# A threshold search moved from ScalarE to VectorE in a sparse-attention decoder layer, and the first query operands made earlier

## The chip, the core and the metric

The kernel runs on one core of one Trainium2 chip. The metric is the device time of one execution in microseconds, the median of several runs. Times inside an execution come from the hardware profile of one run; they are counted from the start of its span.

## What is computed

One decoder layer on 1024 tokens of width 1024 in float32. The part that matters here is the sparse attention. A light indexer gives each query token a score for every earlier token; only the 256 best-scored tokens take part in that query's softmax. The kernel doesn't gather: it finds, for each query row, the exact 256th score as a threshold, and adds a large negative number to the logits of all other tokens.

```python
score = jnp.einsum('bqh,bqhs->bqs', w, jax.nn.relu(logits))
score = jnp.where(causal[None], score, -jnp.inf)
_, idx = lax.top_k(score, k_sel)              # k_sel = 256
s = jnp.where(valid[:, None], s, -jnp.inf)    # s: logits of the chosen tokens
p = jax.nn.softmax(s, axis=-1)
```

Around it stand a modulation of the input, a combined projection (queries, keys, values, pooling channels, indexer), the output projection, two layer norms and a gated feed-forward block.

## The kernel before

The 1024 tokens are eight tiles of 128 rows. Tile i has 128 x (i + 1) earlier tokens; tiles 0 and 1 have 256 at most and need no search. Stages follow each other: the indexer projection, then the scores of tiles 2 to 7 (loop at line 783), then the projections of pooling channels, keys and values in 24 groups (loop at line 940), then attention, output projection, feed-forward.

**The search** (`bisect`, line 627) finds a row's threshold bit by bit: 15 rounds on the upper 16 bits of the score, a short pass in the middle, 16 rounds on the lower 16 bits, then some operations that write the row's bias over its score (lines 709 to 732). A round counts, for each tile of the stream, how many keys lie above a candidate. On VectorE (`search_v`, line 660) a round is one counting pass for each tile (`tensor_scalar` with an accumulated output) and two small updates. On ScalarE (`search_a`, line 672) it is one Sign activation for each tile with an accumulated sum, and four small updates on GpSimd (POOL), which the next round waits for. Lines 37 and 38 share the tiles out: tiles 3 and 2, then 7 and 6, on ScalarE; 5 and 4 on VectorE. A stream's middle and last steps are on VectorE in either case.

**The order of the work.** `fill` (line 761) and `advance` (line 747) are a planner that runs while the program is written. Each engine has an estimated clock; before an operation that would wait, steps of the open streams are put in, if their estimated cost fits into the wait plus a slack (line 51: 0.5 us for VectorE, 1.5 us for ScalarE). Streams opened earlier go first. The stream of 3 and 2 opens in the score loop (line 785), those of 5 and 4 and of 7 and 6 behind it (lines 813, 814). `need(i)` (line 757), called ahead of a tile's first softmax (line 1040), puts in whatever the stream of that tile still lacks.

**Attention** runs over 32 units (group g of two tiles, pair of heads, tile i; line 1020), in the order of tiles 1 and 0, then 3 and 2, 5 and 4, 7 and 6, four pairs of heads each. A unit has its scores on TensorE, a fused add-bias-and-maximum on VectorE and an exponential on ScalarE for each of two heads (`u_exp`, line 1036), a scaling on POOL, transposes on TensorE, copies by ScalarE and VectorE, and the product with the values. Scores and softmax of a unit are put into the program two units ahead of its transposes. From unit 12 on, two steps of another generator are put in with each unit (`mods`, lines 463 and 1145 to 1149): 16 products of 1024 columns and then 8 accumulations, all on VectorE, for the second half's modulation and gate.

**The query operands** (`q_make`, line 1002) are four transposes on TensorE, four copies on ScalarE and two subtractions on VectorE (`q_operands`, line 557). Those of tiles 1 and 0 are made behind the last projection group (lines 1007 to 1015); those of later tiles during attention, at the units listed in `Q_AT` (line 46). Their places (line 991) are in the areas H, W and V. The first two blocks of the output weights (`WO`, line 1096) lie in the area V, from word 4096 to 8192; the first is split by `wo_split(0)` at unit 30 in the program (line 1159).

Of the kernel before, what the change touches and what calls it, by code (L numbers as in the profile page):

```python
# [12 lines left out]
F32R = mybir.dt.float32r  # L13
# [20 lines left out]
BIG = 1.0e30  # L34
NEG = -3.0e38
NOT_TAKEN = -(2.0 ** 100)
TILES_A = ([3, 2], [7, 6])
TILES_V = [5, 4]
PIN = "VAG"
W_POOL = (1, 3)  # L40
AHEAD = 2
# [6 lines left out]
MODS = (12, 2)  # L48
Q_AT = (((0, 0), (1, 0)), ((0, 0), (1, 0)), ((1, 0), (2, 0)))
WARM = 66  # L50
SLACK = {"V": 0.5, "A": 1.5}
SYNC = 0.06
UPDATE = "G"
POOL_AT = 3
# [123 lines left out]
def decoder_layer_kernel(  # L178
# [22 lines left out]
    def buf(where, off, n, name, dt=F32):  # L201
        return nc.alloc_sbuf_tensor_at(f"{name}_{where}{off}", [P, n], dt, offset=area[where] + 4 * off).ap()
# [59 lines left out]
    def raw_slot():  # L262
        n_raw[0] += 1
        return RAW[(n_raw[0] - 1) % 3]
# [286 lines left out]
    def q_transpose(src):  # L551
        pt = psA("qT")
        for pr in range(4):
            T.transpose(pt[:, pr * P : (pr + 1) * P], src[:, pr * P : (pr + 1) * P], ident)
        return pt
# [28 lines left out]
    for c in range(2):  # L584
        pt = psA("ikT")
# [30 lines left out]
    kD = buf("T", 0, 960, "keysD")  # L616
    k4 = buf("T", 960, 320, "keys4")
    k5 = buf("T", 1280, 384, "keys5")
    junkA = buf("X", 6528, 512, "junkA").bitcast(BF16)
    junkB = buf("X", 7040, 256, "junkB").bitcast(BF16)  # L620
    colsD = buf("X", 8576, 64, "colsD")
    keys = {2: kA[:, 0:192], 3: kA[:, 192:448], 4: k4, 5: k5, 6: kD[:, 0:448], 7: kD[:, 448:960]}
    keys = {i: kw.bitcast(I16) for i, kw in keys.items()}
# [3 lines left out]
    def bisect(tiles, cols, on_act):  # L627
# [3 lines left out]
        cntc, kp, sg, cand, pr, M, ng, th, ib, thr, ahead = (col(q) for q in range(11))  # L631
        flip = ib.bitcast(I16)[:, 0:nt]
        kv = {i: keys[i] for i in tiles}
        own = (junkA if 7 in tiles else junkB) if on_act else junk7

        def trash(i):
            return own[:, 0 : P * (i + 1)]
# [100 lines left out]
    def open_stream(*a):  # L738
        pinned.update(PIN)
        b = bisect(*a)  # L740
        streams.append([T.t, next(b), b])
        times.fill = fill
# [40 lines left out]
    for i in range(2, NT):  # L783
# [26 lines left out]
                q_evac(*qpend.pop(0))  # L810
        dg = sc[:, n - P : n]
        G.affine_select(dg, dg, pattern=[[-1, P]], compare_op=ALU.is_ge, fill=NEG, base=0, channel_multiplier=1)
    open_stream(TILES_V, colsD, False)
    open_stream(TILES_A[1], colsA[:, 64:128], True)


    SP.dma_start(pscale, pscale_in)
# [90 lines left out]
    def at_(slot, f):  # L908
        late.setdefault(slot, []).append(f)
# [27 lines left out]

    PAIRS = (0, 6, 8, 14, 16)
    held, pair = {}, None
    for n_, (kind, a, b) in enumerate(groups):  # L940
        if n_ in PAIRS:
            pb = psB("pair")
            held[n_], held[n_ + 1] = pb[:, 0:512], pb[:, 512:1024]
            pair = [(held[q_], u_f(*groups[q_][1:]) if kind == "u" else t_f(groups[q_][1])) for q_ in (n_, n_ + 1)]
        if n_ in held:
            for kp in range(2):
                for pp, f in pair:
                    f(pp, [4 * (n_ not in PAIRS) + 2 * kp, 4 * (n_ not in PAIRS) + 2 * kp + 1])
        else:
            held[n_] = psA("pj")  # L950
            (u_f(a, b) if kind == "u" else t_f(a))(held[n_], range(KT))
        pp = held[n_]
        if n_ in (6, 14):
            w_loads(wk_in if n_ == 6 else wv_in)
        if n_ in (7, 8, 15, 16):
            for kp in ((0, 1) if n_ % 2 else (2, 3)):
                w_split(kp)
        nd = n_ + 2 if n_ in PAIRS else n_ + 1
        if kind == "u":
            at_(nd, lambda a=a, b=b, pp=pp: u_take(a, b, pp))  # L960
            if b == 1:
                at_(nd + 2, lambda a=a: u_split(a))
                at_(nd + 2, lambda a=a: u_split2(a))
                at_(nd + POOL_AT + 1, lambda a=a: u_pool(a))
        elif kind == "k":
            tr = n_ + (4 if n_ in PAIRS or n_ - 1 in PAIRS else 3)
            at_(nd, lambda a=a, pp=pp, tr=tr: take(a, pp, tr))
        else:
            at_(nd, lambda a=a, pp=pp: v_take(a, pp))
        if n_ == 20:  # L970
            at_(n_, lambda: gate_fin(GR, macc, 0, raw_slot()))
        for f in late.pop(n_, []):
            f()
    last = len(groups)
    pinned.clear()

# [6 lines left out]
        n_st[0] = (o + n) % 128 if o + n + n <= 128 else 0  # L983
        return stat[0][:, o : o + n]

    ptb = [[buf("H", (2 * s_ + e) * 2048, 2048, "pT").rearrange("p (j q) -> p j q", j=8) for e in (0, 1)] for s_ in (0, 1)]
    smr = buf("H", 8192, 6144, "sm")
    qabh = buf("H", 14336, 1536, "qab", F32R)
    qabw = [buf("W", 6144 - 2048 * i, 1536, "qab", F32R) for i in (0, 1)]
    qabv = [buf("V", 5120 + i * 1536, 1536, "qab", F32R) for i in (0, 1)]  # L990
    qab = {1: qabh, 0: qabw[0], 3: qabw[1], 2: qabw[0], 5: qabh, 4: qabv[0], 7: qabv[1], 6: qabh}

    qops = {}

    qraw = [buf("C", 768, 512, "qraw"), buf("X", 7552, 512, "qraw")]

    def q_load(i):
        raw = qraw[i % 2]
        SP.dma_start(raw, q_d[i])
        return raw  # L1000

    def q_make(i, raw, pt=None):
        b = qab[i]
        qops[i] = (b[:, 0:1024], b[:, 1024:1536])
        q_operands(pt if pt is not None else q_transpose(raw), *qops[i])

    for s_ in (last, last + 1):
        if s_ == last:
            qr = {i: q_load(i) for i in (1, 0)}
            qp = {i: q_transpose(qr[i]) for i in (1, 0)}  # L1010
        for f in late.pop(s_, []):
            f()
    assert not late, late
    for i in (1, 0):
        q_make(i, qr[i], qp[i])

    def cat_slot(g):
        return WS[g]
# [581 lines left out]
```

## Time and profile before

| | |
|---|---|
| median of 3 runs | 1340.32 us (1337.98 to 1340.81) |
| the profiled execution | 1340.45 us |
| its span | 1338.5 us |
| TensorE matmul busy | 1219.7 us, 91% of the span |
| VectorE (DVE) busy | 1006.4 us, 75% |
| ScalarE (ACT) busy | 592.4 us, 44% |
| GpSimd (POOL) busy | 606.0 us, 45% |
| mean granted TensorE clock | 0.95 |

A share over the whole span is an average over stages with different limits. Stages can be told apart by their rows: projections end at 343.8 us, the first softmax of tile 7 starts at 498.25 us, and from about 550 us on the output projection and the feed-forward block run. In the names, `junkA` is the scratch output of the search of tiles 7 and 6, `junkB` of 3 and 2, `junk` of 5 and 4; `colsA` and `colsD` are the small columns of candidates and counts; `keysD` are the keys of 7 and 6; `qab` is a query operand, `sm` a softmax row, `gacc` the second gate. Line 158 is the helper that issues every operation, so rows are told apart by tile names. [...]

### The profile page before, as it was taken

Reading aid. Unit: us, or ns where it says so; the run is one execution under the profiler, and the core shown is the slowest. Engines: PE = TensorE matmul, PEld = TensorE weight load, DVE = VectorE, ACT = ScalarE, POOL = GpSimd, SP = SyncE. Lnnn points to the kernel's source line nnn. Section 1 sums busy time; section 2 is a strip of 40 time slices with the busy share of each in tenths; the row PEclk is TensorE's granted clock in tenths of the full one; section 3 lists DMA queues with packets and bytes.
Section 4 is the critical chain, followed back from the end, with each engine's and each line's share of the span. In section 5 each row is a group of like instructions: output and inputs, shape, how many; then the busy total and the mean of one; then the engine's idle time right before and its main releaser. Section 6 shows DMA issues by size and latency. Waiting matters only on the chain. (4 is left out here: it accounts for less than half of the span.)

```text
span 1338.5 us, 15961 instructions
## 1 busy us (share of the span) xinstructions
PE 1219.7 (91%) x5570; PEld 958.7 (72%) x5570; DVE 1006.4 (75%) x1685; ACT 592.4 (44%) x1103; POOL 606.0 (45%) x624
## 2 busy tenths in 40 slices
PE   7978997989586849999799999999999999999996
PEld 6655676768454526788677888888888888888875
DVE  6898789889766778467887767576767767676688
ACT  2345754667888956427533223232323223232321
POOL 1393584675344536315663414152342414242557
PEclk8999999989677978999899999999999999999998
DMA  9540020221103431420121011120101112110112
GB/s 337 213 162 31 16 92 19 95 68 44 48 24 118 142 111 64 169 84 1 47 79 63 32 63 63 50 76 33 63 32 64 42 53 70 57 63 32 63 48 110
DMA packets 24997, 101.79 MB, mean 76 GB/s; under 512 B 3411, under 2 KB 3411, under 8 KB 20566
## 3 DMA queue, kind: packets, MB, share of 16 engines
q1 hardware_dynamic: 24918, 100.78, 21.5%
q8 instruction: 44, 0.72, 0.2%
q14 instruction: 35, 0.29, 0.1%
HBM read 92.38 MB, written 8.40 MB: 75 GB/s over the span
## 5 line engine op out<-in xcount | busy, mean ns | idle before, releaser
L158 POOL TENSOR_TENSOR wraw_R<-wraw_R 128x512 f32<-128x512 f32 x44 | 60.1, 1366 | 178.3 <-DVE wblk_T L158 51.3
L158 POOL TENSOR_TENSOR wraw_W<-wraw_W 128x512 f32<-128x512 f32 x44 | 59.5, 1353 | 169.3 <-DVE wblk_V L158 63.8
L158 DVE TENSOR_TENSOR res_X<-res_X,dn 128x512 f32<-128x512 f32 (+1 forms) x145 | 97.4, 680 | 50.9 <-PE dn L158 50.9
L158 PE MATMUL gu<-hr_H,wblk_T 128*128 128x512 f32 (+1 forms) x552 | 125.7, 384 | 3.4 <-ACT stage_W L158 2.6
L158 PE MATMUL gu<-hr_H,wblk_V 128*128 128x512 f32 (+1 forms) x552 | 125.5, 382 | 3.3 <-ACT gtmp_V L158 1.8
L158 PE MATMUL gu<-hr_H,wblk_W 128*128 128x512 f32 (+1 forms) x552 | 125.4, 383 | 0.0
L158 PE MATMUL pj<-ws_W,hT_H 128*128 128x512 f32 x456 | 117.9, 406 | 2.4 <-DVE const_C L158 1.6
L158 PEld LDWEIGHTS gu<-hr_H,wblk_T 128*128 128x128 f32 x552 | 101.7, 191 | 23.7 <-ACT stage_W L158 2.9
L158 PEld LDWEIGHTS gu<-hr_H,wblk_V 128*128 128x128 f32 x552 | 101.0, 189 | 24.0 <-ACT gtmp_V L158 2.0
L158 PEld LDWEIGHTS gu<-hr_H,wblk_W 128*128 128x128 f32 x552 | 101.8, 191 | 19.6
L158 PEld LDWEIGHTS pj<-ws_W,hT_H 128*128 128x128 f32 x456 | 84.5, 191 | 27.6 <-issue 10.2
L158 DVE TENSOR_TENSOR utmp_X<-utmp_X,gu 128x512 f32<-128x512 f32 x88 | 58.2, 682 | 33.5 <-PE gu L158 32.4
L158 DVE TENSOR_TENSOR gtmp_V<-gtmp_V,gu 128x512 f32<-128x512 f32 (+1 forms) x96 | 59.1, 638 | 28.2 <-PE gu L158 28.2
L158 POOL TENSOR_TENSOR colsA_X<-colsA_X 128x2 f32<-128x2 f32 x124 | 40.0, 323 | 80.6 <-ACT junkA_X L158 52.4
L158 POOL TENSOR_SCALAR sm_H<-sm_H,stat_X 128x256 f32<-128x256 f32 (+7 forms) x64 | 53.3, 846 | 50.6 <-DVE stat_X L158 40.1
L158 PE MATMUL dn<-wblk_T,act_W 128*128 128x512 f32 (+1 forms) x294 | 75.1, 385 | 0.0
L158 ACT ACTIVATE junkA_X<-keysD_T,colsA_X 128x1024 bf16<-128x1024 uint16 (+3 forms) x62 | 67.7, 1091 | 15.5 <-POOL colsA_X L158 15.1
L158 PE MATMUL dn<-wblk_V,act_W 128*128 128x512 f32 x288 | 74.4, 389 | 0.0
L158 ACT ACTIVATE act_W<-gtmp_V 128x512 fp32r<-128x512 f32 x40 | 25.3, 633 | 94.9 <-DVE gtmp_V L158 92.9
L158 PE MATMUL gu<-hr_H,wblk_R 128*128 128x512 f32 (+1 forms) x276 | 64.1, 381 | 3.4 <-DVE hr_H L158 3.0
L158 DVE TENSOR_SCALAR_CACHE_REDUCE junk_X<-keys_T,colsD_X 128x768 int16<-128x768 int16 (+1 forms) x64 | 64.3, 1005 | 2.0
L158 PEld LDWEIGHTS dn<-wblk_T,act_W 128*128 128x128 f32 x294 | 54.6, 188 | 11.1
(276 smaller groups left out, 2869.6 us busy)
## 6 DMA issues: line engine op xcount, KB each, us to landing
wm_K<-in_wma_dram SPq DMA_DIRECT2D x16, 512.0 KB, 9.6
raw_R<-in_wmc_dram SPq DMA_DIRECT2D x16, 512.0 KB, 3.7
wraw_R<-in_wg_dram SPq DMA_DIRECT2D x6, 1024.0 KB, 4.7
wraw_R<-in_wd_dram SPq DMA_DIRECT2D x6, 1024.0 KB, 4.8
wraw_W<-in_wup_dram SPq DMA_DIRECT2D x6, 1024.0 KB, 4.8
wraw_R<-in_wup_dram SPq DMA_DIRECT2D x5, 1024.0 KB, 4.8
wraw_W<-in_wg_dram SPq DMA_DIRECT2D x5, 1024.0 KB, 4.8
wraw_W<-in_wd_dram SPq DMA_DIRECT2D x5, 1024.0 KB, 4.8
```

The costliest lines, as they stand in the source:

```text
L158: ins_ = f(*a, **k)
```

## The change

Tile 7 leaves ScalarE's second stream, which keeps tile 6 alone. It becomes a stream of its own on VectorE, opened behind the others, with its own small columns. The slack of ScalarE's fills goes from 1.5 to 1.0 us. The query operands of tiles 1 and 0 are loaded at projection group 17 and made at groups 20 and 21, and now lie in the area V; the operands of the later tiles are shared out anew over H, W and V.

```diff
--- before.py
+++ after.py
@@ -34,8 +34,8 @@
 BIG = 1.0e30
 NEG = -3.0e38
 NOT_TAKEN = -(2.0 ** 100)
-TILES_A = ([3, 2], [7, 6])
-TILES_V = [5, 4]
+TILES_A = ([3, 2], [6])
+TILES_V = ([5, 4], [7])
 PIN = "VAG"
 W_POOL = (1, 3)
 AHEAD = 2
@@ -48,7 +48,7 @@
 MODS = (12, 2)
 Q_AT = (((0, 0), (1, 0)), ((0, 0), (1, 0)), ((1, 0), (2, 0)))
 WARM = 66
-SLACK = {"V": 0.5, "A": 1.5}
+SLACK = {"V": 0.5, "A": 1.0}
 SYNC = 0.06
 UPDATE = "G"
 POOL_AT = 3
@@ -616,8 +616,9 @@
     kD = buf("T", 0, 960, "keysD")
     k4 = buf("T", 960, 320, "keys4")
     k5 = buf("T", 1280, 384, "keys5")
-    junkA = buf("X", 6528, 512, "junkA").bitcast(BF16)
-    junkB = buf("X", 7040, 256, "junkB").bitcast(BF16)
+    junkA = buf("X", 6528, 448, "junkA").bitcast(BF16)
+    junkB = buf("X", 6976, 256, "junkB").bitcast(BF16)
+    colsE = buf("T", 1664, 64, "colsE")
     colsD = buf("X", 8576, 64, "colsD")
     keys = {2: kA[:, 0:192], 3: kA[:, 192:448], 4: k4, 5: k5, 6: kD[:, 0:448], 7: kD[:, 448:960]}
     keys = {i: kw.bitcast(I16) for i, kw in keys.items()}
@@ -631,7 +632,7 @@
         cntc, kp, sg, cand, pr, M, ng, th, ib, thr, ahead = (col(q) for q in range(11))
         flip = ib.bitcast(I16)[:, 0:nt]
         kv = {i: keys[i] for i in tiles}
-        own = (junkA if 7 in tiles else junkB) if on_act else junk7
+        own = (junkA if 6 in tiles else junkB) if on_act else junk7
 
         def trash(i):
             return own[:, 0 : P * (i + 1)]
@@ -810,8 +811,9 @@
                 q_evac(*qpend.pop(0))
         dg = sc[:, n - P : n]
         G.affine_select(dg, dg, pattern=[[-1, P]], compare_op=ALU.is_ge, fill=NEG, base=0, channel_multiplier=1)
-    open_stream(TILES_V, colsD, False)
+    open_stream(TILES_V[0], colsD, False)
     open_stream(TILES_A[1], colsA[:, 64:128], True)
+    open_stream(TILES_V[1], colsE, False)
 
 
     SP.dma_start(pscale, pscale_in)
@@ -937,6 +939,28 @@
 
     PAIRS = (0, 6, 8, 14, 16)
     held, pair = {}, None
+    qr = {}
+    ptb = [[buf("H", (2 * s_ + e) * 2048, 2048, "pT").rearrange("p (j q) -> p j q", j=8) for e in (0, 1)] for s_ in (0, 1)]
+    smr = buf("H", 8192, 6144, "sm")
+    qabh = buf("H", 14336, 1536, "qab", F32R)
+    qabw = buf("W", 6144, 1536, "qab", F32R)
+    qabv = [buf("V", 5120 + i * 1536, 1536, "qab", F32R) for i in (0, 1)]
+    qab = {1: qabv[0], 0: qabv[1], 3: qabh, 2: qabw, 5: qabv[0], 4: qabv[1], 7: qabh, 6: qabv[0]}
+
+    qops = {}
+
+    qraw = [buf("X", 7232, 512, "qraw"), buf("X", 7744, 512, "qraw")]
+
+    def q_load(i):
+        raw = qraw[i % 2]
+        SP.dma_start(raw, q_d[i])
+        return raw
+
+    def q_make(i, raw, pt=None):
+        b = qab[i]
+        qops[i] = (b[:, 0:1024], b[:, 1024:1536])
+        q_operands(pt if pt is not None else q_transpose(raw), *qops[i])
+
     for n_, (kind, a, b) in enumerate(groups):
         if n_ in PAIRS:
             pb = psB("pair")
@@ -969,8 +993,12 @@
             at_(nd, lambda a=a, pp=pp: v_take(a, pp))
         if n_ == 20:
             at_(n_, lambda: gate_fin(GR, macc, 0, raw_slot()))
+        if n_ == 17:
+            qr.update({i: q_load(i) for i in (1, 0)})
         for f in late.pop(n_, []):
             f()
+        if n_ in (20, 21):
+            q_make(21 - n_, qr.pop(21 - n_))
     last = len(groups)
     pinned.clear()
 
@@ -983,36 +1011,10 @@
         n_st[0] = (o + n) % 128 if o + n + n <= 128 else 0
         return stat[0][:, o : o + n]
 
-    ptb = [[buf("H", (2 * s_ + e) * 2048, 2048, "pT").rearrange("p (j q) -> p j q", j=8) for e in (0, 1)] for s_ in (0, 1)]
-    smr = buf("H", 8192, 6144, "sm")
-    qabh = buf("H", 14336, 1536, "qab", F32R)
-    qabw = [buf("W", 6144 - 2048 * i, 1536, "qab", F32R) for i in (0, 1)]
-    qabv = [buf("V", 5120 + i * 1536, 1536, "qab", F32R) for i in (0, 1)]
-    qab = {1: qabh, 0: qabw[0], 3: qabw[1], 2: qabw[0], 5: qabh, 4: qabv[0], 7: qabv[1], 6: qabh}
-
-    qops = {}
-
-    qraw = [buf("C", 768, 512, "qraw"), buf("X", 7552, 512, "qraw")]
-
-    def q_load(i):
-        raw = qraw[i % 2]
-        SP.dma_start(raw, q_d[i])
-        return raw
-
-    def q_make(i, raw, pt=None):
-        b = qab[i]
-        qops[i] = (b[:, 0:1024], b[:, 1024:1536])
-        q_operands(pt if pt is not None else q_transpose(raw), *qops[i])
-
     for s_ in (last, last + 1):
-        if s_ == last:
-            qr = {i: q_load(i) for i in (1, 0)}
-            qp = {i: q_transpose(qr[i]) for i in (1, 0)}
         for f in late.pop(s_, []):
             f()
     assert not late, late
-    for i in (1, 0):
-        q_make(i, qr[i], qp[i])
 
     def cat_slot(g):
         return WS[g]
```

## Rows read from the trace of the kernel before

**Rows 1.** Stage windows: length, busy us (count) by engine, PEclk, DMA share, GB/s

```profile
180.70:343.80 163.10, 149.18 (x646) 120.12 (x644) 150.28 (x291) 94.35 (x185) 106.46 (x170) 0.96 0.21 68
343.80:498.20 154.40, 102.18 (x521) 64.81 (x520) 102.98 (x262) 124.77 (x287) 67.29 (x146) 0.77 0.29 93
375.00:475.00 100.00, 78.08 (x428) 49.34 (x427) 69.21 (x171) 89.05 (x201) 48.60 (x95) 0.85 0.34 110
...
488.00:498.20 10.20, 0.47 (x4) 0.01 (x1) 9.00 (x14) 0.38 (x1) 2.12 (x1) 0.65 0.00 0
498.20:510.00 11.80, 8.31 (x26) 5.81 (x26) 11.48 (x17) 4.82 (x8) 2.85 (x2) 0.50 0.07 20
510.00:540.00 30.00, 29.94 (x184) 19.02 (x183) 21.27 (x41) 21.82 (x41) 23.91 (x16) 0.98 0.23 81
```

**Rows 2.** TensorE's timeline, 343 to 510 us: start, us, operation, [idle before]

```profile
354.41 1.20 PE L158 MATMUL s<-kr_K,qab_H 128*128 128x256 f32 x2 [10.58 <-ACT qab_H L158]
...
499.54 4.37 PE L158 MATMUL s<-kr_K,qab_H 128*128 128x512 f32 x8 [11.07 <-DVE stat_X L158]
```

**Rows 3.** ScalarE's groups by form, 346.6 to 498.2: busy us, mean ns, idle

```profile
L158 ACT ACTIVATE junkA_X<-keysD_T,colsA_X 128x1024 bf16<-128x1024 uint16 x16 | 18.4, 1148 | 7.0 <-POOL colsA_X L158 7.0
...
L158 ACT ACTIVATE junkA_X<-keysD_T,colsA_X 128x1024 bf16<-128x1024 int16 x5 | 5.7, 1148 | 0.9 <-POOL colsA_X L158 0.9
```

**Rows 4.** ScalarE's timeline, the copies of the first query operand

```profile
352.58 2.40 ACT L158 ACTIVATE qab_H<-qT 64x512 fp32r<-64x512 f32 x4
```

**Rows 5.** VectorE's timeline, one round of the search of tiles 5 and 4

```profile
326.61 1.07 DVE L158 TENSOR_SCALAR_CACHE_REDUCE junk_X<-keys_T,colsD_X 128x768 uint16<-128x768 uint16 x1
...
327.73 0.94 DVE L158 TENSOR_SCALAR_CACHE_REDUCE junk_X<-keys_T,colsD_X 128x640 uint16<-128x640 uint16 x1
...
328.71 0.17 DVE L158 TENSOR_SCALAR colsD_X<-colsD_X 128x2 f32<-128x2 f32 x1
...
329.11 1.07 DVE L158 TENSOR_SCALAR_CACHE_REDUCE junk_X<-keys_T,colsD_X 128x768 uint16<-128x768 uint16 x1
```

**Rows 6.** VectorE's groups by form, 346.6 to 498.2: the 1024-wide 16-bit count

```profile
L158 DVE TENSOR_SCALAR_CACHE_REDUCE junkA_X<-keysD_T,colsA_X 128x1024 int16<-128x1024 int16 x1 | 1.3, 1340 | 0.0
```

**Rows 7.** VectorE's timeline in the stall before 498.2, the second gate

```profile
475.99 2.59 DVE L158 SCALAR_TENSOR_TENSOR gacc_V<-raw_R,const_C,gacc_V 128x1024 f32<-128x1024 f32 x2
...
481.00 2.60 DVE L158 SCALAR_TENSOR_TENSOR gacc_V<-raw_R,const_C,gacc_V 128x1024 f32<-128x1024 f32 x2
```

**Rows 8.** VectorE's timeline, first softmax operations of tile 7, then of tile 6

```profile
498.25 1.22 DVE L158 CUSTOM_DVE_ANT_0 sm_H<-s,score_X 128x1024 f32<-128x1024 f32 x1
...
500.47 1.22 DVE L158 CUSTOM_DVE_ANT_0 sm_H<-s,score_X 128x1024 f32<-128x1024 f32 x1
...
508.03 1.09 DVE L158 CUSTOM_DVE_ANT_0 sm_H<-s,score_X 128x896 f32<-128x896 f32 x1
```

**Rows 9.** VectorE's groups by form, 180.7 to 343.8: updates of the search

```profile
L158 DVE TENSOR_SCALAR colsD_X<-colsD_X 128x2 f32<-128x2 f32 x33 | 13.7, 415 | 1.1
...
L158 DVE SCALAR_TENSOR_TENSOR colsD_X<-colsD_X 128x2 f32<-128x2 f32 x31 | 7.6, 246 | 1.1
```

**Rows 10.** VectorE's waits, 180.7 to 343.8: us in total, times, longest

```profile
DVE kr_K L158 <- ACT kr_K L158: 2.7, 1, 2.7
DVE plo_V L158 <- ACT phi_V L158: 2.5, 2, 1.5
DVE wps_X L158 <- ACT wps_X L158: 1.5, 1, 1.5
DVE colsA_X L158 <- POOL colsA_X L158: 0.7, 1, 0.7
```

**Rows 11.** ScalarE's and TensorE's timelines: output weights split, and first used

```profile
517.58 1.07 ACT L158 ACTIVATE wo_V<-raw_R 128x1024 fp32r<-128x1024 f32 x1
...
541.80 0.48 PE L158 MATMUL wo<-wo_V,ws_W 128*128 128x512 f32 x1
```

## The prediction

> **What bounds the kernel now.** I read the stage windows first, because the change touches one third of the span. Between 180.7 and 343.8 us (projections) VectorE is busy 150.3 of 163.1 us and TensorE 149.2; between 343.8 and 498.2 (attention of tiles 1 to 5, ending at the first softmax of tile 7) ScalarE is busy 124.8 of 154.4 us, VectorE 103.0, TensorE 102.2 [rows 1]. The windows inside show ScalarE at 89.05 of 100 us from 375 to 475, then TensorE at 0.47 of 10.2 us before 498.2 [rows 1]. So attention is limited by ScalarE, which carries softmax and the search of tiles 7 and 6, and it ends in a stall: everything waits for tile 7's threshold. After 510 TensorE is busy 29.94 of 30 us [rows 1]; from there the kernel is a fixed train of matrix work, so a shift of tile 7's first softmax is a shift of the end. TensorE's timeline adds one wait at the head of the stage: 10.58 us until 354.41, for ScalarE's copies of the first query operand [rows 2].
>
> **What leaves ScalarE.** 16 and 5 search passes of tile 7 (the 1024-wide form, 1.148 us) run after 346.6 [rows 3], so 21 x 1.148 = 24 us go, and the reads of their accumulators with them. The two query operands go too: four copies are 2.40 us [rows 4], two tiles 4.8 us. ScalarE keeps 124.8 - 24 - 4.8 = 96 us of work in 154 and stops being the limit. Tile 6 alone is searched sooner than the pair was, and nothing waits for it.
>
> **What comes to VectorE.** The same 31 rounds (15 high bits, 16 low bits). A clean round for tiles 5 and 4 together goes from 326.61 to 329.11; its 768-wide pass holds the engine 327.73 - 326.61 = 1.12 us (1.07 plus 0.05), and the two small updates 329.11 - 328.71 = 0.40 [rows 5]. The 1024-wide 16-bit pass took 1.34 us [rows 6]. A round for tile 7 is 1.34 + 0.05 + 0.40 = 1.79 us, the search 31 x 1.79 = **55.5 us**. That is twice what ScalarE gives up, and it lands on an engine that has 154.4 - 103.0 = 51.4 us not busy in the stage.
>
> **The sum**, as VectorE's work from 180.7 (search of 5 and 4 opens) to tile 7's first softmax, for which the kernel before took 317.5 us:
> - busy before: 150.28 + 102.98 = 253.3 [rows 1]. Of this, four accumulations of the second gate (2.59 + 2.60 us [rows 7]) ran early, in the stall: by the unit loop only 20 steps of that generator (16 products and 3 accumulations) stand ahead of tile 7's softmax, and seven accumulations had run. They can follow it, under the TensorE-bound part: 253.3 - 5.2 = 248.0 to count.
> - the search, +55.5.
> - tile 6's last steps. Before, they stand behind tile 7's first softmax: 498.25 to 508.03 less two softmax operations of 1.22 us and small change is 7.2 us [rows 8]. Tile 6 is now finished earlier, so +7.2.
> - the small operations that served tiles 7 and 6 in one go run twice, seven of 0.17 us (estimate): +1.2.
> - stretched small operations. In projections the updates of the search average 415 and 246 ns [rows 9] against 170 in the clean round [rows 5]: 31 x (0.245 + 0.076) = 10 us, where POOL is busy 106.5 of 163.1, 65%; in attention POOL is busy 67.29 of 154.4, 44% [rows 1], with shorter operations. Bounds 0 and 10; I take 2, nearer to the quiet end, since clean rounds are seen even in projections. [...]
> - not busy in projections: 163.1 - 150.3 = 12.8 [rows 1], kept. 7.4 of it are waits on other engines [rows 10]. The new rounds are shorter (1.79 against 2.50), so they fit in smaller gaps: lower bound 8, upper 14.
> - waits left in attention. With VectorE as the limit, it should wait as it does in projections, where it is loaded in the same way: 7.4 of 163.1 is 4.5%, of 154.4 that is 7.0. Lower bound 2; upper bound 17, the 11% that ScalarE, the limit before, was idle from 375 to 475 [rows 1].
>
> 248.0 + 55.5 + 7.2 + 1.2 + 2.0 + 12.8 + 7.0 = 333.7 us, against 317.5: tile 7's softmax comes **16.2 us later**, at about 514.
>
> Given back behind it: with tile 6 done, its softmax no longer stands behind its own search. [...] Net 16.2 - 5 = **+11.2 us**.
>
> The other edits. The early query operands move eight transposes, 4.8 us of ScalarE and four subtractions of VectorE ahead of 343.8. The two loads move four projection groups earlier on SP's queue, ahead of the gate's bias load, beside TensorE's projections; nothing there waits for SP. They remove TensorE's wait of 10.58 us, but that wait is not on VectorE's account: its work only changes sides, so I cost the edit at nothing for the end (bounds -3, should TensorE's head start save waits later, and +3, should the copies delay the last projections' evacuation). The new places of the operands add one wait: tile 6's operand now lies where the first blocks of the output weights are split. That split ran at 517.58, and TensorE used it first at 541.80 [rows 11]; now it waits for tile 6's last scores near the same place relative to the end. 0 to 2 us, taken as 0, since TensorE has other work until then. The smaller slack for ScalarE's fills (1.0 for 1.5) only spreads its rounds; with ScalarE off the limit, nothing. If that cover fails, one late evacuation costs about a round, 1.2 us.
>
> The profiled execution took 1340.45 us (span 1338.5 and 1.95 around it), the median is 1340.32, so no correction: 1340.45 + 11.2 = **1351.7 us**.
>
> **Rivals.**
> - *The search fits (faster).* The place is the projections: VectorE's small updates and splits there are stretched while POOL works; the new order interleaves rounds of two lengths. Should the stretch fall by half of what the updates alone show (5 us of 10), another 3 us go with the splits that share those moments, idle in projections fall to 8 and in attention to 2, the sum is 248.0 + 55.5 + 7.2 + 1.2 - 8 + 8 + 2 = 313.9, so -3.6, and with 5 given back -8.6: 1331.9. It turns faster once work plus waits stay under 317.5 + 5 - 2.7 = 319.8. For it speaks that ScalarE loses 29 us; against it that the sum without any wait in attention is already 326.7.
> - *Even.* Idle 8 and 2, stretch 0, rest as forecast: 321.9, +4.4 - 5 = -0.6: 1339.8.
> - *Hidden badly.* VectorE waits in attention as ScalarE did (17, +10) and its updates are stretched (10, +8): 1351.7 + 18 = 1369.7. [...]
> - *The change does not spread the search.* All rounds stand together ahead of tile 7: the stage without them needs 103.0 - 5.2 + 7.2 = 105.0 us of VectorE, at the 89% that ScalarE reached 118, then 55.5: 343.8 + 173.5 = 517.3, 1355. Close to the forecast, so the sign does not hang on the filling.
>
> **How the numbers follow.** The forecast, with the unspread case, 0.52, its own range 1342 to 1364; badly hidden 0.13; even 0.14; the search fits 0.21. A measurement here can tell about 0.2% (2.7 us). Slower takes the forecast and the bad case, less a little of the forecast's lower edge; same takes the even case and that edge: faster 0.21, same 0.15, slower 0.64. The range runs from 1335, part of the way to the fast case, to 1368.
>
> **What would show it.** Right: from 346 to tile 7's first softmax VectorE busy over 90%, ScalarE under 65%, that softmax at 510 to 518, TensorE's wait at 343.8 gone, and 31 passes of 1024 at 1.34 us on VectorE. The terms are wrong where that softmax comes with VectorE's idle in attention over 17 us or under 2, or where a round is not 1.79. The forecast is wrong if tile 7's softmax comes before 503, or if the part behind it gains more than 7 us.

## The result, and the profile after

Six runs of the changed kernel have a median of **1358.79 us** (1348.55 to 1360.21), six of the kernel before beside them 1340.09 (1337.98 to 1343.05): ratio **1.0123**, 95% interval 1.0089 to 1.0156. The change makes the kernel slower by 1.2%. The profiled execution took 1358.43 us, its span is 1356.5 against 1338.5, so 18.0 us are to be found.

First VectorE's timeline around tile 7's threshold (start, us, operation, in brackets the idle time before).

```profile
500.74 1.33 DVE L158 TENSOR_SCALAR_CACHE_REDUCE junk_X<-keysD_T,colsE_T 128x1024 uint16<-128x1024 uint16 x1
...
502.50 1.34 DVE L158 TENSOR_SCALAR_CACHE_REDUCE junk_X<-keysD_T,colsE_T 128x1024 uint16<-128x1024 uint16 x1
...
504.27 1.34 DVE L158 TENSOR_SCALAR_CACHE_REDUCE junk_X<-keysD_T,colsE_T 128x1024 uint16<-128x1024 uint16 x1
...
505.84 0.96 DVE L158 SCALAR_TENSOR_TENSOR colsE_T<-colsE_T 128x1 f32<-128x1 f32 x1
...
514.72 1.23 DVE L158 CUSTOM_DVE_ANT_0 sm_H<-s,score_X 128x1024 f32<-128x1024 f32 x1
...
519.77 1.09 DVE L158 CUSTOM_DVE_ANT_0 sm_H<-s,score_X 128x896 f32<-128x896 f32 x1 [1.19 <-PE s L158]
```

Tile 7's first softmax comes at 514.72 where it was 498.25 [rows 8]: **+16.5 us of the 18.0**. A round now takes 1.76 us (500.74 to 502.50). Tile 6's softmax follows 5.05 us later; before it was 9.78 [rows 8]. From 514.72 to the end of the span are 841.8 us, before 1338.5 - 498.25 = 840.2. So nearly the whole loss lies ahead of that softmax, and the part behind it is 1.5 us longer.

The stage windows show which engine the stage ran on (length, busy us and count of TensorE, its weight loads, VectorE, ScalarE and GpSimd, granted clock as a share of full speed, DMA share, GB/s).

```profile
180.70:343.80 163.10, 141.07 (x600) 112.96 (x599) 150.23 (x292) 83.91 (x164) 102.03 (x168) 0.94 0.20 67
343.80:514.72 170.92, 114.11 (x556) 74.52 (x555) 155.23 (x399) 100.51 (x244) 69.92 (x142) 0.76 0.24 81
...
500.00:515.00 15.00, 0.00 (x0) 0.00 (x0) 14.23 (x26) 0.00 (x0) 2.34 (x1) 0.63 0.10 36
515.00:530.00 15.00, 13.99 (x37) 8.16 (x37) 8.90 (x17) 8.59 (x15) 4.29 (x4) 0.50 0.10 36
530.00:535.00 5.00, 5.00 (x11) 2.10 (x10) 2.60 (x6) 1.13 (x2) 4.58 (x4) 0.55 0.30 105
535.00:575.00 40.00, 39.59 (x284) 27.74 (x283) 20.81 (x39) 26.55 (x48) 18.42 (x14) 1.00 0.29 106
```

From 343.8 to that softmax VectorE is busy 155.23 of 170.92 us (91%), where it was 103.0 of 154.4, and ScalarE 100.51 (59%) where it was 124.8 [rows 1]. The limit has moved from ScalarE to VectorE. In the last 15 us before the softmax VectorE works almost alone (GpSimd has one operation of 2.34 us). Then TensorE works at a granted clock of 0.50 until about 535; before, this lasted from 498 to about 510 [rows 1].

VectorE's groups by form from 180 to 514.72 give the search's parts (busy us, mean ns, idle before).

```profile
L158 DVE TENSOR_SCALAR_CACHE_REDUCE junk_X<-keysD_T,colsE_T 128x1024 uint16<-128x1024 uint16 x16 | 21.4, 1336 | 0.4
L158 DVE TENSOR_SCALAR_CACHE_REDUCE junk_X<-keysD_T,colsE_T 128x1024 int16<-128x1024 int16 x16 | 21.3, 1333 | 0.2
...
L158 DVE TENSOR_SCALAR colsD_X<-colsD_X 128x2 f32<-128x2 f32 x33 | 13.4, 405 | 1.1
...
L158 DVE SCALAR_TENSOR_TENSOR gacc_V<-raw_R,const_C,gacc_V 128x1024 f32<-128x1024 f32 x6 | 7.6, 1272 | 0.0
L158 DVE SCALAR_TENSOR_TENSOR colsE_T<-colsE_T 128x1 f32<-128x1 f32 x31 | 6.9, 222 | 0.6
...
L158 DVE TENSOR_SCALAR colsE_T<-colsE_T 128x1 f32<-128x1 f32 x35 | 5.2, 149 | 0.5
```

The first accumulation of the second gate (another form, 0.74 us) and the six of the row ran ahead of the softmax, seven of eight. VectorE's waits from 343.8 to 514.72 (total, times, longest) and TensorE's timeline complete the picture.

```profile
DVE stat_X L158 <- ACT sm_H L158: 8.1, 6, 2.2
DVE sm_H L158 <- PE s L158: 1.7, 4, 0.6
DVE ws_W L158 <- ACT ws_W L158: 1.2, 2, 1.0
DVE pT_H L158 <- PE pT L158: 1.1, 2, 0.7
DVE sm_H L158 <- PE pT L158: 0.5, 1, 0.5
DVE sm_H L158 <- POOL colsA_X L158: 0.3, 1, 0.3
```

```profile
333.31 7.28 PE L158 MATMUL pj<-ws_W,hT_H 128*128 128x512 f32 x24 [4.20 <-DVE gr_G L158]
...
351.79 1.33 PE L158 MATMUL s<-kr_K,qab_V 128*128 128x256 f32 x8
...
516.01 3.92 PE L158 MATMUL s<-kr_K,qab_V 128*128 128x512 f32 x8 [17.32 <-DVE stat_X L158]
```

The waits add up to 12.9 us, 8.1 of them reciprocals that wait for ScalarE's exponentials. TensorE's wait of 10.58 us at the head of attention [rows 2] is gone, but its first scores start only 2.6 us sooner (351.79 for 354.41), since the projections end later. Its wait ahead of tile 7 is 17.32 us for 11.07.

### The profile page after: what moved, and what is told of

It is laid out like the page before. It is cut to its first block, busy times and chain, and to the rows that moved or that the text cites. A ratio compares the mean times of both kernels' runs of the same rounds, so it can differ in the third digit from the quotient of the medians.

```text
span 1356.5 us, 16042 instructions
## 1 busy us (share of the span) xinstructions
PE 1225.0 (90%) x5570; PEld 961.8 (71%) x5570; DVE 1055.3 (78%) x1818; ACT 558.9 (41%) x1041; POOL 602.3 (44%) x624
## 5 line engine op out<-in xcount | busy, mean ns | idle before, releaser
L158 POOL TENSOR_TENSOR wraw_W<-wraw_W 128x512 f32<-128x512 f32 x44 | 59.6, 1354 | 169.2 <-DVE wblk_V L158 63.8
L158 PEld LDWEIGHTS pj<-ws_W,hT_H 128*128 128x128 f32 x456 | 85.8, 194 | 33.9 <-issue 11.8
L158 POOL TENSOR_SCALAR sm_H<-sm_H,stat_X 128x256 f32<-128x256 f32 (+7 forms) x64 | 60.5, 957 | 98.5 <-DVE stat_X L158 75.8
L158 PE MATMUL dn<-wblk_W,act_W 128*128 128x512 f32 x240 | 62.2, 389 | 0.0
L158 PEld LDWEIGHTS dn<-wblk_V,act_W 128*128 128x128 f32 x288 | 54.1, 188 | 11.2
```

The lines of the kernel that those rows point to most:

```text
L158: ins_ = f(*a, **k)
```

## The experiments

The table has tile 7's first softmax on VectorE's timeline, the end of the span, the difference of the two, and the ratio of the runs to the kernel before on the same chip. Times in the first three columns are from one profiled execution each, which need not be the median one.

| kernel | softmax | end | behind it | ratio (95%) |
|---|---|---|---|---|
| before | 498.25 | 1338.5 | 840.2 | 1 |
| changed | 514.72 | 1356.5 | 841.8 | 1.0123 (1.0089 to 1.0156) |
| first queries as before | 509.73 | 1346.9 | 837.2 | 1.0103 (1.0069 to 1.0137) |
| first queries alone, kernel before | 503.66 | 1344.1 | 840.4 | 0.9982 (0.9960 to 1.0004) |
| eight rounds fewer | 495.70 | 1332.5 | 836.8 | 0.9972 (0.9948 to 0.9996) |
| modulation behind tile 7 | 480.13 | 1351.9 | 871.8 | 1.0084 (1.0058 to 1.0111) |
| gate first, products behind | 489.37 | 1342.2 | 852.8 | 1.0003 (0.9980 to 1.0026) |
| the same, kernel before | 498.35 | 1354.9 | 856.6 | 1.0107 (1.0071 to 1.0143) |
| TensorE kept busy | 514.78 | 1358.0 | 843.2 | 1.0129 (1.0085 to 1.0173) |
| wider gaps | 502.92 | 1346.8 | 843.9 | 1.0054 (1.0032 to 1.0076) |
| wider gaps, kernel before | 503.22 | 1343.2 | 840.0 | 1.0056 (1.0037 to 1.0076) |
| both moves | 482.77 | 1333.0 | 850.2 | 0.9987 (0.9970 to 1.0003) |
| both moves, kernel before | not read | not read | not read | 1.0071 (1.0047 to 1.0095) |
| tile 6 on VectorE | 498.72 | 1358.7 | 860.0 | 1.0155 (1.0135 to 1.0175) |

**The two halves of the change.** First the early query operands undone:

```diff
-        if n_ == 17:
-            qr.update({i: q_load(i) for i in (1, 0)})
-        if n_ in (20, 21):
-            q_make(21 - n_, qr.pop(21 - n_))
...
+        if s_ == last:
+            qr = {i: q_load(i) for i in (1, 0)}
+            qp = {i: q_transpose(qr[i]) for i in (1, 0)}
...
+    for i in (1, 0):
+        q_make(i, qr[i], qp[i])
```

> The changed kernel with one part undone: the first two query operands (tiles 1 and 0) are made behind the last value projection again, and all query operands lie where the kernel before had them; tile 7's search stays on VectorE. Theory of the prediction (VectorE's work up to tile 7's first softmax sets the end; the place of these operands only moves work from one side of the border to the other and is worth nothing): 1358.8 +-3 us, tile 7's first softmax at 514.7 +-2, TensorE's wait of 10 us before its first attention scores is back, the 4.20 us wait on gr_G at 333 is gone. Rival A (the projections end 8 us later in the changed kernel because of the early operands, and that is what was lost): 1351 to 1354, that softmax at 507 to 510. Rival B (the early operands paid, and hid a part of the search's price): 1362 or more.

TensorE's timeline of this kernel:

```profile
357.49 1.20 PE L158 MATMUL s<-kr_K,qab_H 128*128 128x256 f32 x2 [15.06 <-ACT qab_H L158]
...
511.01 3.92 PE L158 MATMUL s<-kr_K,qab_H 128*128 128x512 f32 x8 [17.32 <-DVE stat_X L158]
```

The wait at the head is back with 15.06 us, and the ratio, 1.0103, lies within the interval of the changed kernel's. The profile is of the shortest of its six runs (1348.81 of a median of 1354.61), so its softmax at 509.73 is no measure of a gain. At 180.7 us its VectorE had 152.53 us of work done for 149.57 in the changed kernel, 3.0 of the 5.0 us. The median is below the 1358.8 +-3 that I expected and just above rival A's range. Then that half alone in the kernel before (the same lines the other way round):

> The kernel before with that one part done alone: first query operands during the last value projections, operand places as in the changed kernel; searches where they were (tiles 7 and 6 on ScalarE, 5 and 4 on VectorE). Theory: here ScalarE sets tile 7's softmax (89 of 100 us busy from 375 to 475); it loses 4.8 us of copies in attention and does them in projections, where it has room: -2 to -5 us, 1335 to 1338. Rival A (the early operands delay the projections by 8 us): +3 to +8, 1343 to 1348. Rival B (TensorE's wait of 10.58 us at the head of attention was on the path): -8 to -10, about 1331.

1338.10 us against 1341.72, ratio 0.9982 (0.9960 to 1.0004). The forecast gain of 2 to 5 us lies inside; none at all does too. Both together: the query operands are worth at most a few us, and the loss comes with the search (or with ScalarE's lower slack, which these two runs move together with it).

**A dose.** Eight rounds fewer on VectorE:

```diff
-        yield from (search_a(16, True) if on_act else search_v(16, ng, True))
+        yield from (search_a(16, True) if on_act else search_v(8 if 7 in tiles else 16, ng, True))
```

> The changed kernel, with the last 8 of the 16 low-bit rounds of tile 7's search left out (its threshold is coarser; nothing else changes). A dose: 8 rounds x 1.79 us = 14.3 us of VectorE work less. Theory (VectorE's work sets tile 7's first softmax): that softmax at 500.4 +-2, end -14 us or some more (TensorE idles less ahead of it): 1341 to 1345. Rival (the search is not spread; only the rounds that stand together right ahead of that softmax count, and from 500.7 to 505.8 these were some three): -5 us at most, 1353 to 1355, and VectorE idles more before.

VectorE's timeline and, below, its groups by form up to there:

```profile
495.70 1.22 DVE L158 CUSTOM_DVE_ANT_0 sm_H<-s,score_X 128x1024 f32<-128x1024 f32 x1
```

```profile
L158 DVE TENSOR_SCALAR_CACHE_REDUCE junk_X<-keysD_T,colsE_T 128x1024 uint16<-128x1024 uint16 x8 | 10.7, 1337 | 0.3
...
L158 DVE SCALAR_TENSOR_TENSOR gacc_V<-raw_R,const_C,gacc_V 128x1024 f32<-128x1024 f32 x4 | 5.1, 1272 | 0.0
```

The softmax moves by 19.0 us, more than the 8 x 1.77 = 14.2 of the dose. Two gate accumulations less ahead of it are another 2.5; the last 2.3 were not traced. The rival (only the three rounds right ahead of the softmax count) allowed 5. The median, 1336.62 us, is below the 1341 to 1345 that I expected. VectorE's work sets that softmax.

**Other work taken away from VectorE.** The modulation generator moved behind tile 7:

```diff
-MODS = (12, 2)
+MODS = (24, 4)
```

> The changed kernel, with the generator of the feed-forward modulation (16 products of 1.26 us, 8 gate accumulations of 1.27, and their loads) started at unit 24 with 4 steps a unit instead of unit 12 with 2, so that all of it stands behind the first softmax of tiles 7 and 6. In the changed kernel the 16 products and 7 accumulations, 20.0 + 8.4 = 28 us of VectorE, ran ahead of that softmax. Theory (VectorE's work counts one for one until another engine limits): that softmax comes 15 to 26 us sooner, at 489 to 500 (TensorE and ScalarE have 114 and 100 us to do from 343.8 to 498.2, so they allow it), and the 28 us fit behind, where VectorE is busy 39 of 75 us from 525 to 600: end 1335 to 1345. Rival A (the products ran in gaps too short for a search round): under 10 us sooner, end 1350 or more. Rival B (the moved work and its 24 loads delay the output projection and the norms): softmax 15 us or more sooner, end within 5 us of 1358.8.

In this kernel a modulation load lands in the slot that holds the first block of the output weights, so the output projection uses partly wrong weights; the amount of work is the same. VectorE's timeline, and TensorE's behind it:

```profile
480.13 1.23 DVE L158 CUSTOM_DVE_ANT_0 sm_H<-s,score_X 128x1024 f32<-128x1024 f32 x1 [0.62 <-PE s L158]
```

```profile
550.13 3.75 PE L158 MATMUL gt<-gacc_V,const_C 128*128 128x512 f32 x4 [14.12 <-DVE gacc_V L158]
```

The softmax comes 34.6 us sooner, more than the 28 us moved, and 30 of these come back behind it: the gate's matmul stands in TensorE's queue and waits 14.12 us for accumulations whose loads are late (by VectorE's timeline the one at 544.36 waits 3.28 us for its load). This is rival B, in kind (median 1353.60, 5.2 us under 1358.8). So the gate was put first and only the products behind. The loop of the accumulations, with the gate's matmul, now stands ahead of the loop of the products; the main lines that change beside that are

```diff
-                SP.dma_start(ring[u], wmc_in[u // 8, u % 8] if u < 16 else wmg_in[1, u - 16])
+                SP.dma_start(ring[u], wmg_in[1, u] if u < 8 else wmc_in[(u - 8) // 8, u % 8])
...
-        acc = buf("V", 4096, 1024, "gacc")
+        acc = buf("X", 5504, 1024, "gacc")
...
-            for _ in range(MODS[1]):
+            for _ in range(1 if n_ < 21 else 4 if n_ >= 22 else 0):
```

> The changed kernel, with the modulation generator turned round: the eight accumulations of the second gate run one a unit from unit 12 (their sum now lies where the first gate's sum lay), and its 16 products run 4 a unit from unit 22, behind the first softmax of tile 7. So 16 x 1.26 = 20 us of VectorE work leave the part ahead of that softmax, and TensorE's matmuls for the gate no longer stand in its queue behind late loads (in the run with all of the modulation behind tile 7 they cost TensorE a wait of 14.12 us). Theory (VectorE's work ahead of tile 7 sets its softmax, and a later one costs more than one for one because TensorE idles into its low clock): softmax at 487 to 497, end 1328 to 1340, under the kernel before. Rival (whatever is moved behind tile 7 comes back there): softmax as said, end 1350 or more.

```profile
489.37 1.23 DVE L158 CUSTOM_DVE_ANT_0 sm_H<-s,score_X 128x1024 f32<-128x1024 f32 x1
```

The row above, of VectorE's timeline, has the softmax where it was expected, 25.4 us sooner. The end is 14.3 sooner, not 20 or more, and the median, 1342.35 us, lies between theory and rival: the products cost 852.8 - 841.8 = 11.0 us behind. The same move in the kernel before is the control:

> The same move (second gate first, the 16 products behind tile 7's first softmax) in the kernel before. Theory: there ScalarE's search sets that softmax and VectorE has 51 us not busy in the stage, so the 20 us that leave are worth little: within 4 us of the kernel before. Rival (VectorE's products were in the way of the search there too, by the waits between passes and updates): 8 us or more faster. Should it come out like that, the changed kernel with this move has no merit of its own.

```profile
498.35 1.23 DVE L158 CUSTOM_DVE_ANT_0 sm_H<-s,score_X 128x1024 f32<-128x1024 f32 x1
```

Here the softmax does not move at all (498.35, by VectorE's timeline; 498.25 before) although VectorE has 13 us less to do from 343.8 on (by the windows, 90.02 us busy for 102.99). That half of the expectation holds: in the kernel before VectorE is not the limit. The other half missed: the products cost 856.6 - 840.2 = 16.4 us behind the softmax (part of it may be the low clock, 0.55 from 500 to 525 there by the windows), and the kernel is 1.1% slower.

**TensorE's clock.** To keep TensorE busy in its wait (`hot` is set while the kernel drives tile 7's search to its end; `burn` makes the transposes that `heat` noted):

```diff
+    def heat(col, n):
+        if hot[0]:
+            w1 = macc[:, 8 * len(hots) : 8 * len(hots) + 8]
+            A.activation(w1[:, 0:1], col, AF.Copy)
+            hots.append((w1, n))
...
+            for _ in range(n):
+                T.transpose(ph[0:8, 0:P], w1, ident)
...
+                heat(one(cntc, 0), 12)
...
                 u_trans(u)
+                burn()
```

> The changed kernel, with TensorE kept busy while it waits for tile 7's first softmax: ScalarE copies a count column of each search round made in that stretch, and TensorE transposes it 12 to 24 times to a place that is not used. In the changed kernel TensorE waits 17.32 us there and then has a granted clock of 0.50 from 515.1 to 545.8 (before: 20.5 us at 0.50). Theory (the head start of tile 6 was given back and then lost again to the low clock): the clock is above 0.9 from 515 on, tile 7's softmax stays at 514 to 517, the end comes 7 to 15 us sooner, 1344 to 1352. Rival (VectorE and ScalarE set the pace behind tile 7, not TensorE's clock): clock up, end within 3 us of 1358.8.

The stage windows of this kernel:

```profile
515.00:520.00 5.00, 3.57 (x21) 2.18 (x20) 3.69 (x8) 3.27 (x7) 1.20 (x2) 1.00 0.56 210
520.00:525.00 5.00, 5.00 (x30) 2.71 (x31) 5.00 (x9) 3.71 (x7) 3.64 (x3) 1.00 0.01 4
525.00:530.00 5.00, 4.06 (x30) 2.73 (x26) 3.43 (x5) 3.03 (x7) 2.33 (x2) 1.00 0.32 105
530.00:535.00 5.00, 3.31 (x7) 1.56 (x8) 4.56 (x8) 1.13 (x2) 2.67 (x3) 0.74 0.31 105
```

The clock is 1.00 from 515 to 530 where it was 0.50, and the end does not move (1.0129), as the rival had it. (The expectation has the low clock of the changed kernel until 545.8; by its windows it ends at about 535.) But the edit moved work too. TensorE's timeline of the changed kernel, then of this one:

```profile
494.65 4.04 PE L158 MATMUL o<-pT_H,vf_V 128*64 128x256 f32 x24
```

```profile
523.60 2.59 PE L158 MATMUL o<-pT_H,vf_V 128*64 128x256 f32 x22
...
531.69 3.01 PE L158 MATMUL gt<-gacc_V,const_C 128*128 128x512 f32 x4 [2.62 <-DVE stat_X L158]
```

The 24 products with the values that the changed kernel did ahead of its wait come behind tile 7's softmax here, and so do ten more transposes and three gate accumulations instead of one. TensorE has idle time instead of a low clock, 4.06 us of the 20 shown, and VectorE is at 5.00 and 4.56 of 5 us in two of the four windows. So this run does not tell what the low clock costs.

The run with the first queries as before does. Behind tile 7's softmax it has the same matmuls as the changed kernel, in nearly the same order and after the same wait of 17.32 us, but its clock came back sooner. Its windows:

```profile
510.00:525.00 15.00, 13.09 (x44) 7.35 (x45) 10.84 (x20) 9.25 (x16) 6.18 (x5) 0.77 0.15 45
525.00:530.00 5.00, 5.00 (x39) 3.66 (x39) 4.86 (x10) 3.93 (x9) 4.57 (x3) 1.00 0.39 132
```

TensorE's timeline of the changed kernel, then of that run:

```profile
531.47 3.49 PE L158 MATMUL gt<-gacc_V,const_C 128*128 128x512 f32 x4
...
538.15 3.46 PE L158 MATMUL o<-pT_H,vf_V 128*64 128x256 f32 x32
```

```profile
523.27 1.96 PE L158 MATMUL gt<-gacc_V,const_C 128*128 128x512 f32 x4 [0.90 <-DVE stat_X L158]
...
528.28 3.92 PE L158 MATMUL o<-pT_H,vf_V 128*64 128x256 f32 x32
```

From the first matmul behind the wait to the products with the values the changed kernel takes 538.15 - 516.01 = 22.1 us, that run 528.28 - 511.01 = 17.3. These 4.9 us are the difference of the parts behind the softmax, 841.8 and 837.2, and a little more. In the changed kernel TensorE is busy 13.99 of 15 and 5.00 of 5 us there, VectorE 8.90 and 2.60. So the low clock does eat tile 6's head start. The six runs of the changed kernel point the same way: the one with the highest mean granted clock, 0.953, took 1348.55 us, the four with 0.940 to 0.942 took 1358.43 to 1360.21. With wider gaps, below, the clock was 0.93 from 500 to 525 and 1.00 from there to 550, and the part behind took 843.9 us, but there five gate accumulations stood in it. Why the clock came back sooner after an equal wait is not shown.

**Wider gaps.** `SLACK = {"V": 1.5, "A": 1.0}` for 0.5, nothing else:

> The changed kernel with VectorE's slack for filling raised from 0.5 to 1.5 us, so that a round of tile 7 (1.79 us, entered at 1.79 by the planner) may be put where an operation would be delayed by up to 1.5 us. From 450 to 475 VectorE was busy 18.2 of 25 us though the search was not done. Theory (work that is put earlier in idle time brings tile 7's softmax forward by the idle time it fills, and delays each softmax it stands ahead of): that softmax 2 to 6 us sooner, end 1350 to 1357. Rival (the delays of the softmax operations run through ScalarE and TensorE and cost what the filling gains): end 1357 to 1363.

```profile
502.92 1.23 DVE L158 CUSTOM_DVE_ANT_0 sm_H<-s,score_X 128x1024 f32<-128x1024 f32 x1
```

The softmax (VectorE's timeline) comes 11.8 us sooner, twice what I expected, and the ratio falls to 1.0054. Idle time was not what was filled: VectorE was not busy for 159.12 - 140.04 = 19.1 us from 343.8 on, against 15.7. The rounds went ahead of other work, and three of eight gate accumulations stood ahead of the softmax where it had been seven. Then the slack alone in the kernel before:

> The kernel before with the slack on VectorE raised from 0.5 to 1.5 us and nothing else. In the changed kernel this gave 9 to 10 us. Theory (the slack brings tile 7's search forward where that search is VectorE's; here VectorE has only tiles 5 and 4, done well before they are needed): within 4 us of the kernel before, 1336 to 1344. Rival (wider slack is a merit of its own): 1334 or less.

There the same slack is a loss of 0.56%, with the softmax 5 us later (VectorE's timeline). The theory allowed 4 us either way, and the median is 7.8 us up. My reading, not traced: tiles 5 and 4 gain nothing from being early, while what stands behind their rounds is delayed. With both moves together, and the products two a unit from unit 24 (beside the lines of the gate first; the two places `srow` and `gacc` are exchanged):

```diff
-SLACK = {"V": 0.5, "A": 1.0}
+SLACK = {"V": 1.5, "A": 1.0}
...
-                ring.append(raw_slot())
+                ring.append(raw_slot() if u < 8 else MRING[u % 2])
...
-            for _ in range(MODS[1]):
+            for _ in range(1 if n_ < 21 or n_ == 22 else 3 if n_ == 24 else 2 if n_ > 24 else 0):
```

> The changed kernel with slack 1.5 on VectorE, the second gate's accumulations one a unit from unit 12, and the 16 modulation products two a unit from unit 24 (their weights land where the search keys lay, so they don't share slots with the output weights). Two moves that each brought tile 7's first softmax forward: 502.9 with the slack, 489.4 with products behind it. Theory (end = tile 7's first softmax + 841 us, plus what the moved work costs behind; four products a unit from unit 22 cost 12.6 us there, two a unit from 24, where VectorE is less busy, should cost under 6): softmax at 478 to 486, end 1324 to 1336, faster than the kernel before. Rival (the products come back in full behind tile 7): 1338 to 1346.

```profile
482.77 1.22 DVE L158 CUSTOM_DVE_ANT_0 sm_H<-s,score_X 128x1024 f32<-128x1024 f32 x1 [0.65 <-PE s L158]
```

The softmax (VectorE's timeline) is as expected (478 to 486), but it now waits for TensorE's scores, and 850.2 us follow it instead of 841.8. The median is 1339.01 us against 1340.39, not the 1324 to 1336 that I expected but in the rival's range: the whole loss of the change is made good, and no more; the version can't be told from the kernel before. The control, both moves in the kernel before:

> The same two moves (slack 1.5, gate first, products two a unit from unit 24) in the kernel before. Theory: ScalarE's search sets tile 7's first softmax there, so it stays at 496 to 500 and nothing is gained; the products behind cost 0 to 8 us (16 with four a unit): 1338 to 1348. Rival (VectorE's load matters there too): softmax before 492, end under 1334.

1350.43 us, ratio 1.0071 (1.0047 to 1.0095): no gain, a little slower than expected. The profile is of an execution of 3010 us and is not read, so where the softmax lay is not known.

**The other tile.** Tiles 7 and 6 exchanged:

```diff
-TILES_A = ([3, 2], [6])
-TILES_V = ([5, 4], [7])
+TILES_A = ([3, 2], [7])
+TILES_V = ([5, 4], [6])
```

> The changed kernel with tiles 7 and 6 exchanged: tile 6's search on VectorE behind tiles 5 and 4, tile 7's on ScalarE alone. A round of tile 6 is 0.13 us shorter, 31 rounds 4 us; tile 7's 31 passes of 1.148 us come back to ScalarE, tile 6's 31 leave it. Theory (VectorE's search sets the end, whichever tile it is, but tile 6's softmax is needed one unit later than tile 7's): tile 7's first softmax at 488 to 500, tile 6's at 505 to 512, end 1346 to 1354. Rival (ScalarE's search, with its update on GpSimd in each round, is again the last to end, as in the kernel before): tile 7's first softmax later than tile 6's threshold, 1340 or 1358 and more by where it ends.

VectorE's timeline, then GpSimd's:

```profile
498.72 1.23 DVE L158 CUSTOM_DVE_ANT_0 sm_H<-s,score_X 128x1024 f32<-128x1024 f32 x1
...
515.58 2.65 DVE L158 TENSOR_TENSOR keysD_T<-keysD_T,score_X 128x896 bf16<-128x896 bf16 x1
...
518.92 2.67 DVE L158 TENSOR_SCALAR score_X<-junk_X 128x896 f32<-128x896 bf16 x1
521.74 1.09 DVE L158 CUSTOM_DVE_ANT_0 sm_H<-s,score_X 128x896 f32<-128x896 f32 x1
```

```profile
515.02 2.72 POOL L158 TENSOR_TENSOR raw_R<-raw_R,gr_G 128x1024 f32<-128x1024 f32 x1 [6.81 <-DMA raw_R<-in_wo_dram]
518.77 2.34 POOL L158 TENSOR_TENSOR raw_R<-raw_R,gr_G 128x1024 f32<-128x1024 f32 x1 [1.03 <-DMA raw_R<-in_wo_dram]
```

Tile 7's softmax is back at 498.72, yet the kernel is the slowest of all by its ratio; I had expected tile 6's softmax at 505 to 512 and the end at 1346 to 1354, and the rival's mechanism did not come either. Tile 6's softmax comes at 521.74, and 1358.7 - 521.74 = 837.0 follow it; in the changed kernel tile 6's stood at 519.77, with 1356.5 - 519.77 = 836.7 behind. So a late threshold of tile 6 is paid for as one of tile 7 is. Five gate accumulations (1.28 us each) stood between tile 6's last steps, and two of those took 2.65 and 2.67 us where they took 0.61 and 0.73 in the changed kernel.

## Why the prediction was right, and where it was not

**Sign and size: right.** Forecast 1351.7, in a range of 1335 to 1368; measured 1358.79. VectorE became the limit, its search of tile 7 sets the end, and the dose, the removed products and the control in the kernel before show it.

**Tile 7's softmax: right, by terms that offset each other.** Forecast +16.2, measured +16.5; that it fits to 0.3 us is luck. By the same account from 180.7 to the softmax the forecast had 313.9 us of work and 19.8 not busy. The windows have 150.23 + 155.23 = 305.5 busy and 12.9 + 15.7 = 28.6 not busy.
- *Rounds:* 1.76 us for 1.79, and the count 1.33 to 1.34. Right.
- *Stretched updates:* the second update averages 222 ns against 159 in the median, 31 x 0.063 = 2.0 us. Right, and the first update (149 ns) is not stretched at all. The bounds were 0 and 10; the trace decides for the low end.
- *Gate accumulations, -5.2:* wrong. Seven of eight still ran ahead of the softmax. I took the unit loop's order for the engine's order. Where they did stay behind (five of them with the wider gaps, three with eight rounds fewer) the softmax gained more than the rounds explain.
- *Waits left in attention, 7.0:* too small. The view gives 12.9 us of waits and 15.7 not busy, inside the bounds of 2 to 17 but near the top. I took VectorE's waits in projections as the pattern. In attention it waits for ScalarE's exponentials (8.1), which projections do not have.
- *Busy time:* with the accumulations put back, the forecast's work is 319.1, 13.6 over the measured. I added rounds by their spacing (1.76) to a sum of merged busy time, in which a round counts 1.65 (500.74 to 502.08, 502.12 to 502.27, 502.31 to 502.47): 3 to 4 us. Another 2.3 ran before 180.7. Some 7 us are not traced.

**Given back behind it, 5: wrong, and the step that failed.** Tile 6's softmax did follow 4.7 us closer, as priced, but the part behind tile 7's softmax is 1.5 us longer, not 5 shorter. No run shows the 5: it was my estimate, between 508.03 - 503.9 = 4.1 us (tile 6's softmax [rows 8] less the end of its scores, 499.54 + 4.37 [rows 2]) and the 7.2 us of its last steps [rows 8]; in its place the runs showed these 4.7 and 1.5. I counted tile 6's scores at the low clock and put nothing for what came behind them. But the granted clock stayed at 0.50 until about 535, some 20 us from that softmax, where before it had lasted until about 510, some 12 [rows 1]; and in that stretch TensorE was busy almost without a gap (13.99 of 15 us and 5.00 of 5) and set the pace. In two runs whose clock was up sooner the part behind is shorter than in the kernel before: by 3.0 us with the first queries as before (clock 0.77 from 510 to 525, then 1.00), by 3.4 with eight rounds fewer (clock 1.00 from 500 to 525). So the mechanism was there, at less than 5 us, and the longer low clock took it. What keeps the clock low for longer is left open. With the softmax right to 0.3 us, this term is the miss: 5 + 1.5 of the 18.0 - 11.2 = 6.8 us between forecast and measurement.

**Query operands at nothing: right**, within the few us that the two runs can tell. The lower **slack** of ScalarE was not tried alone. The **output weights** cost what was said: TensorE waits 0.41 us at its second use of them, at 560.21.

**Rivals.** The unspread case (1355) is near the number but not the mechanism: by the groups three rounds ran in projections, 28 in attention, and only three of these stood together at its end. The fast case needed VectorE idle 10 us in all; it was 28.6.

## What to carry to other kernels

Before moving work to an engine with room, add up its work to the point where the result is needed, and ask what else stands ahead of that point and could stand behind. Here 28 us of modulation could, but it had a price behind, and it paid only for the engine that had become the limit; the same move, and the same planner slack, were a loss in the kernel before. Take the order on the engine from the trace, not from the loop that issues it. And where TensorE waits for the result, count what it then does at the low clock: here, at 0.50 for some 20 us, that ate what was given back behind the wait.

## What the runs showed of the hardware

An update of one column was stretched in one form only: the one with two inputs. In the changed kernel the 128x1 TENSOR_SCALAR stayed at 126 to 155 ns in all its executions, while the 128x2 form averaged 405 ns with 2378 at most; the SCALAR_TENSOR_TENSOR was stretched at one column too, up to 1137 ns, as at 505.84 above, where it ended at 506.80 and GpSimd's multiplication at 504.45 + 2.34 = 506.79. The one-column TENSOR_SCALAR just ahead of it ran in the middle of that multiplication and took its usual time (VectorE's timeline, then GpSimd's):

```profile
505.65 0.15 DVE L158 TENSOR_SCALAR colsE_T<-colsE_T 128x1 f32<-128x1 f32 x1
```

```profile
504.45 2.34 POOL L158 TENSOR_TENSOR raw_R<-raw_R,gr_G 128x1024 f32<-128x1024 f32 x1 [13.15 <-DMA raw_R<-in_wo_dram]
```

In the run with tiles 7 and 6 exchanged both long steps ended within 0.5 us of GpSimd's multiplications (518.23 and 517.74; 521.59 and 521.11).

The update at 505.84 and the step of 2.65 us read two tensors; the step of 2.67 us reads one, and so does the 128x2 TENSOR_SCALAR. So the number of inputs alone does not tell which operations are stretched, and no run shows why the 128x1 TENSOR_SCALAR was not.
